# A hybrid decoder step on one core: in which order the weight sums are made, and which engine does the small two-operand arithmetic

## The chip, the core and the metric

The kernel runs on one core of a Trainium2 chip. A core has a matrix engine (TensorE, PE in the profile), VectorE (DVE), ScalarE (ACT), GpSimd (POOL) and a queue engine (SyncE, SP); each works through its own list of instructions in order and waits on semaphores for the others. PEld is TensorE's loading of weights, DMA the transfer engines that move data between DRAM and the core's memory. DMAs are issued from SP and, the adding ones in this kernel, from GpSimd. The metric is the time of one execution on the device in microseconds; the time before is the median of three runs.

## The reference

One layer with two token mixers beside each other, over 512 prompt tokens and 8 x 4 sampled tokens (544 columns in all), in float32:

```python
z = x @ w_in                                   # 1024 -> a_val, a_gate, b_x, b_gate, g_a, g_b
u = a_val * jax.nn.sigmoid(a_gate)
ua = jnp.concatenate([ctx_a, u], axis=1)
ca = jax.nn.silu(layer_norm(causal_dwconv(ua, w_dw_a, b_dw_a), ln_a_g, ln_a_b))   # 31 taps
y_a = ca @ w_proj_a
ub = jnp.concatenate([ctx_b, b_x], axis=1)
cb = causal_dwconv(ub, w_dw_b, b_dw_b)                                            # 4 taps
hs, h_last = rg_lru(cb, h0, w_rg_a, b_rg_a, w_rg_x, b_rg_x, rg_lam, reset_first)
y_b = (hs.astype(x.dtype) * jax.nn.gelu(b_gate)) @ w_proj_b
mix = (jax.nn.sigmoid(g_a) * y_a + jax.nn.sigmoid(g_b) * y_b) @ w_out
x1 = layer_norm(DN_ALPHA * x + mix, ln1_g, ln1_b)
ff = jnp.square(jax.nn.relu(x1 @ w_ff1)) @ w_ff2
ple = jax.nn.sigmoid(x1 @ w_ple_gate) * (p @ w_ple_proj)
y = layer_norm(DN_ALPHA * x1 + ff + ple, ln2_g, ln2_b)
```

In `rg_lru`, r and ig are sigmoids of two block-diagonal products of cb; a = exp(-8 r softplus(-lam)), the input is sqrt(1 - a^2) * ig * cb, and h is the running sum h = a h + input over the tokens.

## The kernel before

Channels lie on the 128 partitions and tokens along the free axis, so one channel tile is 128 x 544. Every matrix product is made of three passes over operands that are split into a high and a low part: ScalarE copies a weight chunk `raw` (128 x 1024) to `hi`, VectorE subtracts to get `lo`, and TensorE multiplies hi by hi, hi by lo and lo by hi. One chunk feeds 48 matmuls.

The order of the products is the string `ORDER`: "a" is the gated input of the 31-tap convolution, "x" that of the 4-tap one, "r" the two block-diagonal products (two groups of five channel tiles), "g", "b" and "c" the gates, "p" the product with `w_proj_b` and "q" that with `w_proj_a`. Then come `w_out`, the first layer norm, the embedding gate, the feed-forward layers (FF below) and the last norm.

Beside the products run steps that VectorE, ScalarE and GpSimd take when a planner finds room. `Clocks` keeps a modelled time for each engine, `put` hands in a sequence of steps with a priority and a due chunk, `fill` takes the next ones up to 1.5 us ahead of TensorE's modelled time, and `need` forces what is due. The list that each engine then works through is fixed when the program is built. The largest such work is `queue_conv_a`: for each of the eight channel tiles, four `products` (128 x 248) with two sums over them for the sampled tokens, then 30 taps (`tap`, ca<-u,par_a,ca, 128 x 482 to 511) on VectorE for the prompt tokens. `last` adds the finished tile to `sum_a`. When all eight are in, `lna` (the convolution's layer norm) starts: `lnash` and `lnasl` are the split of sum_a, and lnamu is the matmul on TensorE that makes the mean. The chain from there to `cas`, the input of "q", runs while TensorE does the rest of "p" and part of the gates.

`conv_b_sample` makes the 4-tap convolution of the sampled tokens (tiles cbs, seven instructions of 128 x 64 and two of 128 x 32 for two channel tiles). `rg_group` multiplies the sigmoid `gg` by `cb` as soon as ScalarE has made it, and `scan` multiplies `gate` by the scan's result. Two-operand arithmetic in all of these is issued on GpSimd (`G`), beside its small copies (ctx_a, ctx_b, tb, st_u, hl).

The feed-forward layers are done with seven products in place of eight, for which some weight blocks are sums of others (S3, S1, S2, S4). These sums are made in DRAM beside the earlier stages: a DMA from SP copies one block to a scratch tile, and a DMA from GpSimd (`accum_op=add`) adds a second block, S3 for S2, and S2 for S4. There are 92 of them. `sum_stream` says when: the k-th add falls due when TensorE's modelled time reaches `SUM_FROM + k * SUM_EVERY`, and its copy `COPY_AHEAD` adds earlier. The feed-forward stage loads the sums as `fraw<-sum_S`.

```python
def sum_stream(e):
    k = (clocks.t["T"] - SUM_FROM) / SUM_EVERY
    if e == "D" and to_copy and n_adds - len(to_copy) < k + COPY_AHEAD:
        return 0.0, copy_one
    if e == "G" and to_add and len(to_copy) < len(to_add) and n_adds - len(to_add) < k:
        return 0.0, add_up
```

All compute is issued through one helper, so nearly every row of the profile carries line L155; rows are told apart by tile names.

Of the kernel before, what the change touches and what calls it, by code (L numbers as in the profile page):

```python
# [20 lines left out]
CK, RK = 31, 4  # L21
# [12 lines left out]
PANELS = [(1, p, None) for p in (1, 2, 3)]  # L34
for _g, _ps in enumerate(((4, 5, 6), (7, 8, 9), (10, 11, 12, 13), (14, 15))):
    PANELS += [(2, _p, _g) for _p in range(4)] + [(1, _p, None) for _p in _ps]
SUM_FROM, SUM_EVERY, COPY_AHEAD = 40.0, 6.0, 3
RAW_BUFS = 3
SPLIT_BUFS = 4
LOAD_AHEAD = 5  # L40
# [119 lines left out]
def tile_hybrid_step(ctx: ExitStack, tc: tile.TileContext, I, O):  # L160
# [72 lines left out]

    lead = [LEAD]
    sums, summed_up, to_copy, to_add = {}, set(), deque(), deque()
    for kind, n in [(1, p) for p in (1, 2, 3)] + [(2, p) for p in range(4)] + [(1, p) for p in range(4, 16)]:
        w = I["w_ff1" if kind == 1 else "w_ff2"][n]
        ncol = 512 if kind == 1 else 6 * P
        for c in range(kind):
            cs = slice(c * ncol, c * ncol + ncol)  # L240
            s = {nm: dpool.tile([P, ncol], F32, name=f"sum{kind}_{n}_{c}_{nm}") for nm in ("S3", "S1", "S2", "S4")}
            for nm, own, src in (("S3", w[0, :, cs], w[2, :, cs]), ("S1", w[2, :, cs], w[3, :, cs]),
                                 ("S2", w[3, :, cs], s["S3"]), ("S4", w[1, :, cs], s["S2"])):
                sums[kind, n, c, nm] = s[nm]
                to_copy.append(lambda to=s[nm], own=own: DMA.dma_start(to, own))
                to_add.append((lambda to=s[nm], src=src: G.dma_start(to, src, accum_op=OP.add, max_dma_last_dim=1024),
                               (kind, n, c, nm)))
    n_adds = len(to_add)

# [463 lines left out]

    sg, u, ca = [None] * 8, [None] * 8, [None] * 8
    sum_a = [None]

    todo = []

# [15 lines left out]
    def queue_conv_a(ct):  # L734
        def wk(k):
            return par_a[:, k, ct:ct + 1]
        prod = {}

        def products():
            for t in range(NS):  # L740
                if t % 2 == 0:
                    prod[t // 2] = apool.tile([P, NB, 2, CK], F32, tag="act", name=f"prod{ct}_{t}")
                G.tensor_mul(prod[t // 2][:, :, t % 2, :], ctx_a[ct // 2][:, ct % 2, :, t:t + CK],
                             par_a[:, 0:CK, ct].unsqueeze(1).to_broadcast([P, NB, CK]))

        def reduce(t):
            cv = conv_s[:, ct, :].rearrange("p (b t) -> p b t", t=NS)
            V.tensor_reduce(cv[:, :, 2 * t:2 * t + 2], prod[t], op=OP.add, axis=AX.X)

        def first():  # L750
            ca[ct] = act(f"ca{ct}")
            S.activation(ca[ct][:, :SEQ], u[ct][:, :SEQ], AF.Identity, scale=wk(CK - 1), bias=A("b_dw_a", ct))
            S.activation(ca[ct][:, SEQ:], conv_s[:, ct, :], AF.Identity, bias=A("b_dw_a", ct))

        def tap(k):
            s = CK - 1 - k
            V.scalar_tensor_tensor(ca[ct][:, s:SEQ], u[ct][:, :SEQ - s], wk(k), ca[ct][:, s:SEQ],
                                   op0=OP.mult, op1=OP.add)

        def last():  # L760
            if sum_a[0] is None:
                sum_a[0] = act("sum_a")
                G.tensor_copy(sum_a[0], ca[ct])
            else:
                G.tensor_add(sum_a[0], sum_a[0], ca[ct])

        may_start = lambda: 0.0 if len(summed) >= ct // 2 * 2 - 1 else INF
        steps = [("G", products, may_start), ("V", lambda: reduce(0)), ("V", lambda: reduce(1)), ("S", first)]
        steps += [("V", lambda k=k: tap(k)) for k in range(CK - 1)]
        put(3 + 0.1 * (ct // 2), steps + [("G", last)] + [("V", lambda: summed.append(ct))],  # L770
            PROJ_A - CONV_DUE)

    summed = []
# [70 lines left out]
    def conv_b_sample(c0):  # L844

        ws = R_OFF["w_dw_b"]
        acc_, t = (cpool.tile([P, 2, NB, NS], F32, tag=f"cbs{i}", name=f"cbs{i}_{c0}", bufs=1) for i in range(2))
        for k in range(RK):
            w = par_r[:, ws + k, c0:c0 + 2].unsqueeze(2).unsqueeze(3).to_broadcast([P, 2, NB, NS])
            G.tensor_mul(t if k else acc_, ctx_b[:, c0:c0 + 2, :, k:k + NS], w)  # L850
            if k:
                G.tensor_add(acc_, acc_, t)
        for j in range(2):
            G.tensor_scalar(cb[c0 + j][:, SEQ:].rearrange("p (b t) -> p b t", t=NS), acc_[:, j], R("b_dw_b", c0 + j),
                            None, op0=OP.add)

    tb = cpool.tile([P, 10, RK - 1], F32, name="tb")
# [11 lines left out]
    def rg_group(g):  # L869
        b0 = 5 * g  # L870

        def prod(mt, w, isx):
# [10 lines left out]
            else:  # L883
                gg[ct] = act(f"gg{ct}")
                S.activation(gg[ct], tok(ps), AF.Sigmoid, bias=R("b_rg_x", ct))
                G.tensor_mul(gg[ct], gg[ct], cb[ct])
            fill()

        def decay_act(mt):
# [10 lines left out]
        def scan(mt):  # L900
# [4 lines left out]
            def last():  # L905
                V.tensor_tensor_scan(sq[ct], aa[ct], gg[ct], 0.0, op0=OP.mult, op1=OP.add)
                G.tensor_copy(hl[:, ct, :], sq[ct][:, SEQ - 1::NS])
                G.tensor_mul(gate[ct], gate[ct], sq[ct])

            def part(p):  # L910
                if p == 0:
# [137 lines left out]

    def evac_proja(mt, ps, h):  # L1050
        V.tensor_mul(sa[mt], tok(ps), sa[mt])
        (G if mt < 6 else V).tensor_add(sa[mt], sa[mt], sb[mt])

        def keep(parts_):
            mix[mt] = parts_
# [663 lines left out]
```

## Time and profile before

| | us |
|---|---|
| three runs | 1013.59, 1014.58, 1017.05 |
| median | 1014.58 |
| the profiled execution | 1010.48 |
| its span, first to last instruction | 1008.7 |
| TensorE busy | 935.5 (93%) |
| VectorE busy | 793.7 (79%) |
| ScalarE busy | 496.1 (49%) |
| GpSimd busy | 254.2 (25%) |

Busy is time with at least one instruction in the engine. The profile is of one execution, 4.1 us faster than the median of the runs. Instructions of one engine overlap at their ends: a row's mean duration is longer than the spacing of a run of such instructions.

### The profile page before, as it was taken

To read this page: it belongs to the slowest core of one execution; us is meant where nothing else is said; L and a number is where in the kernel's file an instruction comes from. 1 tells how busy PE (TensorE), PEld (TensorE's weight loads), DVE (VectorE), ACT (ScalarE), POOL (GpSimd) and SP (SyncE) were. 2 spreads that over 40 slices of the span, in tenths; PEclk is the share of its full clock that TensorE was granted. 3 is DMA by queue.
4 is the path that set the end of the run, shared out by engine and by line. 5 is a ranking of instruction groups with operands and counts; after the bars stand their busy time and mean duration, and the time that the engine had idled before them with its cause. 6 is when DMAs were issued, how large, how long until landed. Compare 5 with 4: busy or idle time off the path is not lost.

```text
span 1008.7 us, 18589 instructions
## 1 busy us (share of the span) xinstructions
PE 935.5 (93%) x7236; PEld 924.7 (92%) x7236; DVE 793.7 (79%) x1337; ACT 496.1 (49%) x875; POOL 254.2 (25%) x265
## 2 busy tenths in 40 slices
PE   8999798975989797999999999999999999999895
PEld 8999798975979797999999999989999899989895
DVE  5799999899997998793356883979688686777547
ACT  6422236623449622562233772775674655854601
POOL 0453755675637621210421211000000000000002
PEclk9999988997989899999999999999999999999998
DMA  8557689875889594967869784446546446446412
GB/s 298 147 152 185 180 200 262 196 175 138 183 214 202 136 212 130 229 160 196 260 155 253 173 225 54 149 133 188 174 138 204 148 146 218 147 144 204 133 48 84
DMA packets 125272, 175.81 MB, mean 174 GB/s; under 512 B 9920, under 2 KB 97344, under 8 KB 124224
## 3 DMA queue, kind: packets, MB, share of 16 engines
q1 hardware_dynamic: 96064, 146.31, 45.0%
q0 software_dynamic: 29120, 28.32, 20.3%
q8 instruction: 57, 0.93, 0.4%
q14 instruction: 31, 0.25, 0.1%
HBM read 167.57 MB, written 60.44 MB: 226 GB/s over the span
## 4 chain that ended last, share of the span: by engine, by line
PE 47%; DVE 29%; DMA 7%; ACT 7%; issue 5%; POOL 4%; SPq 0%; DVEq 0%; POOLq 0%; ACTq 0%
PE psq L155 13%; PE ps L155 13%; DVE ca L155 11%; PE f L155 8%; PE g L155 6%; DVE lo L155 4%; ACT fy L155 2%; ACT fhi L155 1%; DMA fraw<-sum_S 1%; DMA sum_S<-in_w_ff_dram 1%; DVE flo L155 1%; PE pps L155 1%; DVE th L155 1%; ACT fz L155 1%; DMA sum_S<-sum_S 1%
## 5 line engine op out<-in xcount | busy, mean ns | idle before, releaser
L155 DVE SCALAR_TENSOR_TENSOR ca<-u,par_a,ca 128x482 f32<-128x482 f32 (+29 forms) x240 | 176.3, 792 | 0.3
L155 ACT ACTIVATE hi<-raw 128x1024 fp32r<-128x1024 f32 (+3 forms) x109 | 99.9, 929 | 130.3 <-PE ps L155 52.6
L155 ACT ACTIVATE fhi<-fraw 128x512 fp32r<-128x512 f32 (+1 forms) x229 | 124.3, 571 | 60.5 <-DMA fraw<-sum_S 21.7
L155 DVE TENSOR_TENSOR flo<-fraw,fhi 128x512 fp32r<-128x512 f32 (+1 forms) x229 | 138.2, 620 | 17.7 <-ACT fhi L155 17.4
L155 DVE TENSOR_TENSOR lo<-raw,hi 128x1024 fp32r<-128x1024 f32 (+3 forms) x105 | 122.2, 1178 | 25.4 <-ACT hi L155 25.4
L155 POOL TENSOR_TENSOR y<-y,rows_g 128x512 f32<-128x512 f32 x2 | 3.1, 1550 | 379.1 <-ACT y L155 379.1
L155 POOL DMA_DIRECT2D sum_S<-sum_S x46 | 45.3, 985 | 171.5 <-DMA sum_S<-sum_S 91.2
L155 PE MATMUL f<-x1h,fhi 128*128 128x272 f32 x212 | 59.6, 294 | 5.1 <-DVE fz L155 3.5
L155 POOL DMA_DIRECT2D sum_S<-in_w_ff_dram x46 | 51.8, 1198 | 28.5 <-DMA sum_S<-in_w_ff_dram 27.1
L155 PE MATMUL f<-x1h,flo 128*128 128x272 f32 x212 | 58.6, 289 | 0.2 <-DVE flo L155 0.2
L155 PE MATMUL f<-x1l,fhi 128*128 128x272 f32 x212 | 58.4, 288 | 0.0
L155 PE MATMUL ps<-x0h,hi 128*128 128x288 f32 x104 | 23.9, 313 | 29.6 <-ACT gate L155 14.6
L155 PEld LDWEIGHTS ps<-x0h,hi 128*128 128x128 f32 x104 | 16.9, 200 | 31.5 <-ACT gate L155 15.5
L155 PEld LDWEIGHTS f<-x1h,fhi 128*128 128x128 f32 x212 | 39.0, 189 | 7.3 <-DVE fz L155 5.4
L155 DVE TENSOR_TENSOR acc<-acc,g 128x272 f32<-128x272 f32 x80 | 34.8, 434 | 12.9 <-PE g L155 12.1
L155 PEld LDWEIGHTS f<-x1h,flo 128*128 128x128 f32 x212 | 38.9, 188 | 0.5 <-DVE flo L155 0.5
L155 PEld LDWEIGHTS f<-x1l,fhi 128*128 128x128 f32 x212 | 39.0, 189 | 0.0
L155 PE MATMUL psq<-x1l,hi 128*128 128x288 f32 (+1 forms) x128 | 36.9, 288 | 0.0
L155 PE MATMUL psq<-x1h,lo 128*128 128x288 f32 (+1 forms) x128 | 36.8, 288 | 0.0
L155 PE MATMUL psq<-x1h,hi 128*128 128x288 f32 (+1 forms) x128 | 36.8, 288 | 0.0
L155 POOL TENSOR_TENSOR prod<-ctx_a,par_a 128x248 f32<-128x248 f32 x32 | 30.9, 1150 | 0.0
L155 ACT ACT_TABLE_LOAD x20 | 25.7, 1283 | 1.1 <-PEq L1709 0.7
(1994 smaller groups left out, 3385.9 us busy)
## 6 DMA issues: line engine op xcount, KB each, us to landing
raw<-in_w_in_dram SPq DMA_DIRECT2D x51, 512.0 KB, 5.0
fraw<-in_w_ff_dram SPq DMA_DIRECT2D x65, 256.0 KB, 3.5
sum_S<-in_w_ff_dram SPq DMA_DIRECT2D x60, 256.0 KB, 5.3
fraw<-sum_S SPq DMA_DIRECT2D x60, 256.0 KB, 3.3
sum_S<-in_w_ff_dram SPq DMA_DIRECT2D x32, 384.0 KB, 5.8
fraw<-sum_S SPq DMA_DIRECT2D x64, 192.0 KB, 2.9
fraw<-in_w_ff_dram SPq DMA_DIRECT2D x48, 192.0 KB, 3.1
sum_S<-in_w_ff_dram POOLq DMA_DIRECT2D x30, 256.0 KB, 5.4
```

Source lines behind the costliest of these rows:

```text
L155: return fn(out, *args, **kw)
```

## The change

The constants of the sums change, and their order: panels are taken in seven sets of three or four, and within a set all S3 are made, then all S1, all S2 and all S4. The two-operand instructions of GpSimd go to VectorE, all but four at the very end of the program. The first tile of `sum_a` is no longer copied: the first add takes two tiles.

```diff
-SUM_FROM, SUM_EVERY, COPY_AHEAD = 40.0, 6.0, 3
+SUM_FROM, SUM_EVERY, COPY_AHEAD = 25.0, 7.2, 4
...
-    for kind, n in [(1, p) for p in (1, 2, 3)] + [(2, p) for p in range(4)] + [(1, p) for p in range(4, 16)]:
...
+    SETS = ([(1, p, 0) for p in (1, 2, 3)], [(2, p, 0) for p in range(4)], [(1, p, 0) for p in (4, 5, 6)],
+            [(1, p, 0) for p in (7, 8, 9)], [(2, p, 1) for p in range(4)], [(1, p, 0) for p in (10, 11, 12)],
+            [(1, p, 0) for p in (13, 14, 15)])
+    for ps_ in SETS:
+        for nm in ("S3", "S1", "S2", "S4"):
+            for kind, n, c in ps_:
...
-                G.tensor_mul(prod[t // 2][:, :, t % 2, :], ctx_a[ct // 2][:, ct % 2, :, t:t + CK],
+                V.tensor_mul(prod[t // 2][:, :, t % 2, :], ctx_a[ct // 2][:, ct % 2, :, t:t + CK],
...
             if sum_a[0] is None:
+                first_ca.append(ct)
+                sum_a[0] = True
+            elif sum_a[0] is True:
                 sum_a[0] = act("sum_a")
-                G.tensor_copy(sum_a[0], ca[ct])
+                V.tensor_add(sum_a[0], ca[first_ca[0]], ca[ct])
             else:
-                G.tensor_add(sum_a[0], sum_a[0], ca[ct])
+                V.tensor_add(sum_a[0], sum_a[0], ca[ct])
...
-        steps = [("G", products, may_start), ("V", lambda: reduce(0)), ("V", lambda: reduce(1)), ("S", first)]
+        steps = [("V", products, may_start), ("V", lambda: reduce(0)), ("V", lambda: reduce(1)), ("S", first)]
...
-            G.tensor_mul(t if k else acc_, ctx_b[:, c0:c0 + 2, :, k:k + NS], w)
+            V.tensor_mul(t if k else acc_, ctx_b[:, c0:c0 + 2, :, k:k + NS], w)
             if k:
-                G.tensor_add(acc_, acc_, t)
+                V.tensor_add(acc_, acc_, t)
...
-            G.tensor_scalar(cb[c0 + j][:, SEQ:].rearrange("p (b t) -> p b t", t=NS), acc_[:, j], R("b_dw_b", c0 + j),
+            V.tensor_scalar(cb[c0 + j][:, SEQ:].rearrange("p (b t) -> p b t", t=NS), acc_[:, j], R("b_dw_b", c0 + j),
...
-                G.tensor_mul(gg[ct], gg[ct], cb[ct])
+                V.tensor_mul(gg[ct], gg[ct], cb[ct])
...
-                G.tensor_mul(gate[ct], gate[ct], sq[ct])
+                V.tensor_mul(gate[ct], gate[ct], sq[ct])
...
-        (G if mt < 6 else V).tensor_add(sa[mt], sa[mt], sb[mt])
+        V.tensor_add(sa[mt], sa[mt], sb[mt])
```

First place: GpSimd's list in the first 50 us, before and then after. A row `sum1_2_0_S3<-in_w_ff1_dram` is the adding DMA of form S3 of panel 2; `S2<-...S3` reads an earlier sum.

```order
L155 DMA sum1_1_0_S3_101<-in_w_ff1_dram 256x256
L155 DMA sum1_1_0_S1_102<-in_w_ff1_dram 256x256
L155 DMA sum1_1_0_S2_103<-sum1_1_0_S3_101 256x256
L155 COPY st_u_269<-u2_801 128x30
L155 COPY ctx_a1_260<-u2_801 128x8x4
L155 COPY st_u_269<-u3_833 128x30
L155 COPY ctx_a1_260<-u3_833 128x8x4
L155 DMA sum1_1_0_S4_104<-sum1_1_0_S2_103 256x256
```

```order
L155 DMA sum1_3_0_S1_106<-in_w_ff1_dram 256x256
L155 COPY ctx_b_264<-bx0_935 128x8x4
L155 COPY tb_284<-bx0_935 128x3
L155 COPY ctx_b_264<-bx1_970 128x8x4
L155 COPY tb_284<-bx1_970 128x3
L155 DMA sum1_1_0_S2_107<-sum1_1_0_S3_101 256x256
L155 DMA sum1_2_0_S2_108<-sum1_2_0_S3_102 256x256
L155 DMA sum1_3_0_S2_109<-sum1_3_0_S3_103 256x256
```

Before, an S2 stands one add behind the S3 that it reads, and the next copies behind that; after, five adds lie between a panel's S3 and its S2.

Second place: VectorE's list at the first group of block-diagonal products, before and then after. `u` is the last convolution input, `lo` and `hi` of 128x896 and 32x384 the split of the group's second weights.

```order
L155 TENSOR_TENSOR u_1891<-ps_1_1758,sg_1755 128x544
L155 TENSOR_TENSOR lo_1909<-raw_1724,hi_1824 128x896
L155 TENSOR_TENSOR hi_1895<-raw_1769,hi_1895 32x384
L155 SCALAR_TENSOR_TENSOR ca_1417<-u_801,par_a,ca_1417 128x495
L155 SCALAR_TENSOR_TENSOR ca_1594<-u_833,par_a,ca_1594 128x493
```

```order
L155 TENSOR_TENSOR u_1881<-ps_1_1748,sg_1745 128x544
L155 TENSOR_TENSOR gg_1896<-gg_1896,cb_939 128x544
L155 TENSOR_TENSOR gg_1913<-gg_1913,cb_974 128x544
L155 TENSOR_TENSOR gg_1931<-gg_1931,cb_1375 128x544
L155 TENSOR_TENSOR gg_1947<-gg_1947,cb_1410 128x544
L155 TENSOR_TENSOR gg_1961<-gg_1961,cb_1537 128x544
L155 TENSOR_TENSOR lo_1964<-raw_1694,hi_1816 128x896
L155 TENSOR_TENSOR hi_1885<-raw_1757,hi_1885 32x384
```

The five multiplies that stood on GpSimd's list now stand in a row on VectorE's, ahead of the next weight split; the second group has the same five.

Third place: TensorE's list around lnamu, before and then after.

```order
L155 MATMUL ps_0_4359<-hb6h,lo_4300 128x256
L155 MATMUL lnamu_4454<-lnash,ones 128x288
L155 MATMUL lnamu_4454<-lnasl,ones 128x288
L155 MATMUL lnamu_4460<-lnash,ones 128x256
L155 MATMUL lnamu_4460<-lnasl,ones 128x256
L155 MATMUL ps_0_4359<-hb7h,hi_4227 128x288
```

```order
L155 MATMUL ps_0_4497<-hb6h,lo_4523 128x256
L155 MATMUL lnamu_4590<-lnash,ones 128x288
L155 MATMUL lnamu_4590<-lnasl,ones 128x288
L155 MATMUL lnamu_4594<-lnash,ones 128x256
L155 MATMUL lnamu_4594<-lnasl,ones 128x256
L155 MATMUL ps_0_4497<-hb7h,hi_4399 128x288
```

The mean's four matmuls stand at row 2660 of TensorE's list before and at row 2780 after: 120 matmuls of "p" go ahead of them. All other rows of TensorE keep their order, but for the four of the variance, which move back likewise.

## Rows read from the trace of the kernel before

**Rows 1.** Windows: busy us and counts by engine, TensorE's clock, DMA, four stages.
```profile
0.00:40.00 40.00, 37.32 (x276) 36.48 (x277) 21.21 (x29) 23.24 (x30) 8.69 (x22) 1.00 0.68 234
40.00:400.30 360.30, 316.51 (x2402) 313.40 (x2400) 341.64 (x465) 155.96 (x212) 191.16 (x191) 0.94 0.78 184
400.30:620.00 219.70, 219.08 (x1719) 218.22 (x1720) 144.75 (x259) 101.52 (x182) 48.10 (x50) 0.99 0.79 196
620.00:1008.70 388.70, 362.62 (x2845) 356.62 (x2844) 286.05 (x586) 215.39 (x452) 6.30 (x4) 0.99 0.47 147
```
**Rows 2.** Waits of TensorE, 100 to 400.5 us: total, times, longest.
```profile
PE ps L155 <- ACT gate L155: 14.6, 3, 12.1
...
PE lnamu L155 <- ACT lnash L155: 6.3, 1, 6.3
```
**Rows 3.** Windows, the same columns: behind two of TensorE's waits, and an undisturbed stretch.
```profile
126.30:132.20 5.90, 5.89 (x26) 5.89 (x27) 5.90 (x9) 4.60 (x7) 4.34 (x7) 0.50 0.98 185
...
400.30:405.40 5.10, 5.10 (x21) 4.90 (x22) 5.10 (x13) 3.43 (x8) 1.41 (x3) 0.50 0.71 143
60.00:100.00 40.00, 40.00 (x321) 40.00 (x321) 40.00 (x56) 12.43 (x15) 19.69 (x25) 1.00 0.69 172
```
**Rows 4.** Timeline of VectorE, 80 to 92 us: start, length, instruction, count.
```profile
80.44 0.71 DVE L155 TENSOR_TENSOR cb1l<-cb,cb1h 128x544 fp32r<-128x544 f32 x1
81.07 3.97 DVE L155 SCALAR_TENSOR_TENSOR ca<-u,par_a,ca 128x496 f32<-128x496 f32 x6
```
**Rows 5.** Timeline of VectorE, 154 to 165 us.
```profile
156.03 9.31 DVE L155 SCALAR_TENSOR_TENSOR ca<-u,par_a,ca 128x495 f32<-128x495 f32 x6
```
**Rows 6.** Timeline of GpSimd, 154 to 165 us.
```profile
155.56 8.61 POOL L155 TENSOR_TENSOR gg<-gg,cb 128x544 f32<-128x544 f32 x5
```
**Rows 7.** GpSimd by operation, 33.4 to 401 us: busy, mean ns, idle before.
```profile
L155 POOL TENSOR_TENSOR prod<-ctx_a,par_a 128x248 f32<-128x248 f32 x32 | 30.9, 1150 | 0.0
...
L155 POOL TENSOR_TENSOR gate<-gate,th 128x544 f32<-128x544 f32 x10 | 19.8, 1980 | 0.0
L155 POOL TENSOR_TENSOR gg<-gg,cb 128x544 f32<-128x544 f32 x10 | 18.1, 1841 | 11.8 <-ACT gg L155 11.8
...
L155 POOL COPY ctx_b<-bx 128x32 f32<-128x32 f32 x10 | 15.2, 1521 | 9.1 <-ACT bx L155 9.1
L155 POOL TENSOR_TENSOR sum_a<-sum_a,ca 128x544 f32<-128x544 f32 x7 | 12.5, 1781 | 15.5 <-DVE ca L155 14.4 <-DVE aa L155 1.0
```
**Rows 8.** Timeline of VectorE, 104 to 112 us.
```profile
105.19 5.34 DVE L155 SCALAR_TENSOR_TENSOR ca<-u,par_a,ca 128x510 f32<-128x510 f32 x2
```
**Rows 9.** Timeline of VectorE, 218 to 246 us.
```profile
222.89 5.27 DVE L155 TENSOR_TENSOR t<-aa,par_r 128x8 f32<-128x8 f32 x1
...
242.95 0.17 DVE L155 TENSOR_TENSOR t<-aa,par_r 128x8 f32<-128x8 f32 x1
```
**Rows 10.** Timeline of VectorE, 400 to 405 us.
```profile
402.10 1.51 DVE L155 TENSOR_TENSOR ca<-ca,lnamu 128x288 f32<-128x288 f32 x4
```
**Rows 11.** Waits of VectorE, 40 to 400.5 us: total, times, longest.
```profile
DVE conv_s L155 <- POOL prod L155: 4.0, 2, 3.0
DVE lnasl L155 <- ACT lnash L155: 3.1, 1, 3.1
```
**Rows 12.** Tile gg, 140 to 175 us: duration ns min/median/max, first and last start.
```profile
L155 ACT ACTIVATE gg<-rg,par_r x5: 704/715/717, 151.4 to 157.8; 128x544 f32<-128x544 f32 x5
```
**Rows 13.** Timeline of GpSimd, 28 to 36 us.
```profile
29.55 0.21 POOL L155 COPY st_u<-u 128x30 f32<-128x30 f32 x1 [28.05 <-DVE u L155]
```
**Rows 14.** Timeline of GpSimd, 178 to 192 us.
```profile
180.32 5.68 POOL L155 COPY ctx_b<-bx 128x32 f32<-128x32 f32 x1 [1.80 <-ACT bx L155]
```
**Rows 15.** Waits of all engines, whole span.
```profile
POOL sum_S L155 <- DMA sum_S<-sum_S: 91.2, 16, 9.9
```
**Rows 16.** Windows, columns as above: either side of the feed-forward stage's start.
```profile
560.00:620.00 60.00, 60.00 (x484) 60.00 (x484) 45.12 (x100) 36.15 (x81) 11.96 (x14) 1.00 0.77 178
620.00:680.00 60.00, 56.30 (x439) 54.77 (x439) 48.26 (x99) 39.32 (x85) 0.00 (x0) 1.00 0.40 118
```

More of the change, by code (lines that the diff above doesn't have):

```diff
@@ L235, in tile_hybrid_step @@
     sums, summed_up, to_copy, to_add = {}, set(), deque(), deque()
-    for kind, n in [(1, p) for p in (1, 2, 3)] + [(2, p) for p in range(4)] + [(1, p) for p in range(4, 16)]:
[L237 to L246, printed above, removed]
+    SETS = ([(1, p, 0) for p in (1, 2, 3)], [(2, p, 0) for p in range(4)], [(1, p, 0) for p in (4, 5, 6)],
[4 more added lines that the diff above has]
+            for kind, n, c in ps_:
+                w = I["w_ff1" if kind == 1 else "w_ff2"][n]
+                ncol = 512 if kind == 1 else 6 * P
+                cs = slice(c * ncol, c * ncol + ncol)
+                s = sums[kind, n, c, nm] = dpool.tile([P, ncol], F32, name=f"sum{kind}_{n}_{c}_{nm}")
+                own, src = {"S3": (0, w[2, :, cs]), "S1": (2, w[3, :, cs]), "S2": (3, sums.get((kind, n, c, "S3"))),
+                            "S4": (1, sums.get((kind, n, c, "S2")))}[nm]
+                to_copy.append(lambda to=s, own=w[own, :, cs]: DMA.dma_start(to, own))
+                to_add.append((lambda to=s, src=src: G.dma_start(to, src, accum_op=OP.add, max_dma_last_dim=1024),
                                (kind, n, c, nm)))
@@ L715, in tile_hybrid_step @@
     sum_a = [None]
+    first_ca = []
     todo = []
@@ L761, in last @@
             if sum_a[0] is None:
+                first_ca.append(ct)
+                sum_a[0] = True
+            elif sum_a[0] is True:
                 sum_a[0] = act("sum_a")
-                G.tensor_copy(sum_a[0], ca[ct])
+                V.tensor_add(sum_a[0], ca[first_ca[0]], ca[ct])
             else:
-                G.tensor_add(sum_a[0], sum_a[0], ca[ct])
+                V.tensor_add(sum_a[0], sum_a[0], ca[ct])
         may_start = lambda: 0.0 if len(summed) >= ct // 2 * 2 - 1 else INF
-        steps = [("G", products, may_start), ("V", lambda: reduce(0)), ("V", lambda: reduce(1)), ("S", first)]
+        steps = [("V", products, may_start), ("V", lambda: reduce(0)), ("V", lambda: reduce(1)), ("S", first)]
         steps += [("V", lambda k=k: tap(k)) for k in range(CK - 1)]
-        put(3 + 0.1 * (ct // 2), steps + [("G", last)] + [("V", lambda: summed.append(ct))],
+        put(3 + 0.1 * (ct // 2), steps + [("V", last)] + [("V", lambda: summed.append(ct))],
             PROJ_A - CONV_DUE)
```

## The prediction

> **What bounds the kernel now.** I read the windows by stage first, then TensorE's waits, then VectorE's and GpSimd's timelines beside each other. In the feed-forward stage and from 400 to 620 us TensorE is busy 363 of 389 and 219 of 220 us [rows 1]: little is to be had there. The loss is from 40 to 400 us: TensorE is busy 316.5 of 360.3 us, idle 43.8, and VectorE is busy 341.6 [rows 1]. At full clock TensorE did 321 matmuls in 40 us, 8.03 per us [rows 3], so its 2402 matmuls [rows 1] need 299 us; it took 61 us more. Most of the difference is waiting: 12.1 us at one place for a chain that ends in gate, 6.3 us at the end for lnash [rows 2]. The rest is the clock: after each of six such waits the granted clock was 0.50, the 1.2 GHz level, for some us more (5.9 us behind the first, 5.1 behind the last) [rows 3].
>
> Why VectorE is full is the second reading. Six taps in a row took 3.97 us when GpSimd did no arithmetic, so 0.65 each [rows 4]. Six taps beside five gg multiplies took 9.31 us [rows 5], while the five took 8.61 us [rows 6]: the two engines alternated, and each multiply cost VectorE (9.31 - 3.97)/5 = 1.07 us. The four products of one tile did the same: two taps took 5.34 us [rows 8], 4.0 more than their own 1.3, and a small multiply of 0.17 us took 5.27 [rows 9] with products and a sum_a add beside it. So work put on GpSimd here is paid by VectorE, at more than VectorE's own price: a subtraction of the same 128 x 544 takes 0.63 us there (start to start, 80.44 to 81.07) [rows 4].
>
> So the end of this stage is set by VectorE's list up to lnamu, and I count on that list.
>
> **The change part by part.** All terms go against the profiled execution, 1010.48 us (span 1008.7 and 1.8 around it); the median of the runs is 4.1 us longer, which I add at the end.
>
> *Stalls that go.* gg: 10 x 1.07 = 10.7 us. gate: 10 of like size and mean length [rows 7], some beside idle time of VectorE: 9. sum_a: 7 adds, 7. Products: 32 in eight groups of four [rows 7]; two groups come before 40 us, one met a VectorE that was waiting for it [rows 11], the other five at 2.7 to 4.0 (the upper end from [rows 8]): 17. Together 44, bounds 38 and 50. VectorE's own work up to lnamu is then 341.6 - 44 = 297.6 us.
>
> *Work that comes to VectorE.* 24 products of 128 x 248 behind 40 us: four subtractions of 256 and 288 columns took 1.51 us [rows 10], so 0.33 each, 7.9. The eight earlier ones fall where VectorE is busy 21 of 40 us [rows 1] and cost nothing; that cover gone, 2.6. The 45 small ones of conv_b_sample: 8 columns take 0.17 [rows 9], 544 take 0.71 [rows 4], about 1 ns a column between them; for 32 and 64 columns 0.2, as most wait for the one before: 9. The 27 of 128 x 544 (10 gg, 10 gate, 7 sum_a): 0.66, 17.8. Together 35, bounds 31 and 42. The six adds on `sa` fall behind 460 us, where VectorE has room: nothing (4 us if it had not).
>
> *lnamu stands 120 matmuls later on TensorE.* That takes 120/8.03 = 14.9 us of work out of what follows lnamu, and puts some three more weight splits and evictions ahead of it on VectorE: 3 us.
>
> *Waits.* VectorE was idle 360.3 - 341.6 = 18.7 us, and its waits name GpSimd or a ScalarE step behind a GpSimd one: 4.0 on products, 3.1 on lnash behind sum_a [rows 11], and ScalarE's halves of cb behind cbs. These mostly go. New ones come, as VectorE's list is in order. In each of the two groups five gg multiplies stand ahead of the next weight split; ScalarE made the five gg over 151.4 to 157.8 us and 0.7 [rows 12], 7.1 us against 3.2 of multiplies: up to 3.9 us of waiting, behind which lo and the taps stand, and TensorE waits for lo. And cbs now waits on VectorE for GpSimd's copy ctx_b, five times, 0.7 each. I take 12 us of idle time in all (8 and 3.5 and a remainder), bounds 1.3 and 55 (below).
>
> *lnamu.* It comes at 40 + 297.6 + 35 + 3 + 12 = 387.6 us against 400.3: 12.7 earlier. TensorE could have been there at 40 + 2522/8.03 = 354, so VectorE still sets it. With the 14.9 us, and 2.6 for the half clock behind lnamu (5.1 us at 0.50 [rows 3]) when the long wait is gone, 30.2 us. The norm's chain behind lnamu has 55 us of matmuls as cover before "q" needs it (counted in the order), 70 before; TensorE, busy 219 of 220 us there [rows 1], was never kept by it. I cost it at nothing; if it comes late, 5.
>
> *The order of the sums.* GpSimd stood 91.2 us for an S3 or S2 of the same panel [rows 15]. Nothing on another engine waits for an add itself, so its end brings only that the copies queued behind are not held up. Ten adds now come after the feed-forward stage has begun, over 538 matmuls or 67 us, where there were none; in the order each sum is first loaded 180 us or more of matmuls behind its add, so none is late. But they share the DMA: 0.77 busy before the stage's start, 0.40 behind it [rows 16]. With sums in it I expect about 0.8 there, as in the first stage, and weight loads that come later, as SP's list has the sums' copies between them: 2 us, bounds 0 and 8. At the start three copies go ahead of SP's sixth weight chunk; with DMA busy 0.68 up to 40 us [rows 1] and five chunks ahead of it that costs nothing, or 3.
>
> Sum: 1010.5 - 30.2 + 2 = 982.3; at the median, 986.
>
> **A rule against the change.** The alternation above has five multiplies of 8.61 us beside six taps [rows 5, 6]. The Trainium skill, SBUF — State Buffer, "Who interferes with whom", has it that a VectorE instruction with two SBUF inputs and a GpSimd instruction that reads SBUF hold a shared port in turn, each for its whole length, and the later one is blocked. By that rule the copies left on GpSimd, which read SBUF too, are held off all the more when VectorE has 35 us more of such work; the trace agrees: a copy of 0.21 us beside an idle VectorE [rows 13], and one of 5.68 [rows 14].
>
> **Rivals.** *The copies hold VectorE.* ctx_b's ten copies took 15.2 us [rows 7], and cbs now waits for them on VectorE. Against it: VectorE is late and rarely there first, and while it waits a copy is short. If they count in full: 986 + 15 = 1001.
>
> *TensorE nearly bounds the stage.* All waits of VectorE go but 1.3 us of gaps, the stalls were 50 and the new work 31: lnamu at 40 + 291.6 + 31 + 3 + 1.3 = 367, 20.7 earlier than above, no loss on the sums: 963. For it: most waits named GpSimd; against it: the five gg in a row.
>
> *VectorE takes over GpSimd's waits.* This is the slower side. GpSimd waited 11.8 us for gg and 9.1 for bx [rows 7]; on VectorE nobody would do taps meanwhile. With these in full, the copies' 15.2 and its old 18.7, idle time is 54.8, 42.8 more than I took: 1029. It becomes slower than before from 40 us of idle time on, over twice what there is now. Against it: GpSimd was early for those waits, and VectorE will be late.
>
> *Nothing is won.* The stage's end is set by weight loads and clock, not by VectorE: 1012 to 1017. Against it: VectorE is 95% busy and its stalls are plain.
>
> **How the numbers follow.** My forecast 0.62, with its own range 972 to 1000; copies 0.15; TensorE bound 0.10; VectorE waits 0.08; nothing 0.05. The range 964 to 1008 holds the first three but their outer ends, and leaves out the last two. No change, within 0.3% (3 us, about what can be told apart here), is 0.05; slower 0.08; faster 0.87.
>
> **What would show it.** Right: taps at 0.65 us each throughout to lnamu, VectorE busy some 335 us from 40 us to lnamu and lnamu at about 388; GpSimd busy under 100 us; no wait for a sum of the same panel; VectorE idle a few us at each row of five gg. Wrong: lnamu later than 400; waits of VectorE for GpSimd's copies; long waits of TensorE for fhi from 590 to 660 us.

## The result, and the profile after

The changed kernel takes 1005.08 us (median of 4 runs, 1004.12 to 1007.80) against 1014.09 us for the kernel before beside it: a ratio of 0.991, 95% interval 0.988 to 0.994. It is faster, by 9 us where 28 were forecast. The profiled execution took 1004.12 us, its span 1002.3.

The page and the windows of the changed kernel, in the columns of [rows 1], with the stages cut at the new lnamu (399.1 us) and at the new first matmul of the feed-forward layers (f0). f0 was at 627.7 and is at 616.4; [rows 1] cuts at 620, so the last line is the stretch from lnamu to f0 in the kernel before:

```profile
PE 938.7 (94%) x7236; PEld 927.5 (93%) x7236; DVE 794.6 (79%) x1447; ACT 493.5 (49%) x874; POOL 139.1 (14%) x154
...
0.00:40.00 40.00, 37.81 (x274) 36.50 (x275) 20.61 (x47) 23.23 (x30) 5.88 (x18) 1.00 0.89 280
40.00:399.10 359.10, 329.39 (x2522) 326.68 (x2521) 342.87 (x557) 156.78 (x216) 86.22 (x89) 0.96 0.71 172
399.10:616.40 217.30, 209.97 (x1657) 208.89 (x1655) 147.64 (x266) 99.75 (x183) 31.86 (x33) 0.99 0.76 187
616.40:1002.30 385.90, 361.52 (x2788) 355.48 (x2788) 283.47 (x581) 213.77 (x448) 15.09 (x14) 0.97 0.54 161
```
```profile
400.30:627.70 227.40, 225.79 (x1774) 224.72 (x1775) 146.96 (x265) 103.24 (x187) 48.10 (x50) 0.99 0.77 190
```

GpSimd is at 86 us in the second stage, under the 100 that were to show the move right, and TensorE does 2522 matmuls from 40 us to lnamu, 120 more than before, as the order said. But lnamu is at 399.1, not at 387.6. VectorE was busy 342.9 us where 335.6 were forecast (7.3 more) and idle 359.1 - 342.9 = 16.2 us where I took 12 (4.2 more): together the 11.5 us. And from lnamu to f0 it took 217.3 us, 10.1 less than before and not 17.5 less: TensorE, which was idle for 227.4 - 225.8 = 1.6 us of that stretch before, was idle for 7.3.

VectorE's list from 40 to 400 us by operation (busy us, mean ns of one, idle before; the mean counts the overlap with the next instruction, the busy time does not):

```profile
L155 DVE SCALAR_TENSOR_TENSOR ca<-u,par_a,ca 128x482 f32<-128x482 f32 (+28 forms) x240 | 160.3, 734 | 0.2
L155 DVE TENSOR_TENSOR prod<-ctx_a,par_a 128x248 f32<-128x248 f32 x32 | 18.7, 658 | 0.0
L155 DVE TENSOR_TENSOR gate<-gate,th 128x544 f32<-128x544 f32 x10 | 7.3, 725 | 0.3
L155 DVE TENSOR_TENSOR gg<-gg,cb 128x544 f32<-128x544 f32 x10 | 7.1, 723 | 4.3 <-ACT gg L155 4.3
L155 DVE TENSOR_TENSOR cbs<-ctx_b,par_r 128x64 f32<-128x64 f32 x20 | 4.0, 222 | 3.4 <-POOL ctx_b L155 3.0
```

Every tap now costs about what an undisturbed one cost in [rows 4]: 160.3/240 = 0.67 us each. The two rows of five gg cost 4.3 us of waiting together, the copies of ctx_b 3.0. What is off is one line: 32 products, not 24 (none came before 40 us), at 18.7/32 = 0.58 us each, not 0.33.

What VectorE (40 to 399 us) and TensorE (120 to 400 us) waited for in the changed kernel (us in total, times, longest), and what GpSimd did before the longest of these waits, 161.6 to 170.2 us:

```profile
DVE lo L155 <- ACT hi L155: 6.6, 2, 4.2
...
PE rg L155 <- ACT th L155: 9.3, 2, 8.6
```
```profile
124.54 3.69 POOL L155 DMA_DIRECT2D sum_S<-in_w_ff_dram  x3
146.53 0.64 POOL L155 COPY st_u<-u 128x30 f32<-128x30 f32 x1 [18.31 <-DVE u L155]
147.11 0.70 POOL L155 COPY ctx_a<-u 128x32 f32<-128x32 f32 x1
149.72 0.64 POOL L155 COPY st_u<-u 128x30 f32<-128x30 f32 x1 [1.90 <-DVE u L155]
150.30 0.70 POOL L155 COPY ctx_a<-u 128x32 f32<-128x32 f32 x1
150.95 4.95 POOL L155 DMA_DIRECT2D sum_S<-in_w_ff_dram  x4
153.96 2.95 POOL L155 DMA_DIRECT2D sum_S<-sum_S  x1
```

GpSimd stood 18.3 us in front of a copy whose input VectorE had not made yet and 1.9 us in front of the next one, and the five adds that stood behind them all went out at once. The DMAs issued from 145 to 175 us landed so late (KB each, median us from issue to landing):

```profile
raw<-in_w_in_dram SPq DMA_DIRECT2D x4, 512.0 KB, 15.0
sum_S<-in_w_ff_dram POOLq DMA_DIRECT2D x4, 384.0 KB, 13.4
...
sum_S<-sum_S POOLq DMA_DIRECT2D x1, 384.0 KB, 22.1
```

A load of these weights (`raw`, 512 KB) takes 5.1 us in the median of the whole run; here it took 15. `th`, for which TensorE waited, stood on ScalarE behind the split (`hi`) of such a load. The same happens at the output projection, on GpSimd and then on VectorE:

```profile
510.43 0.42 POOL L155 COPY sum<-res 128x288 f32<-128x288 f32 x1 [25.31 <-DVE res L155]
510.90 3.86 POOL L155 DMA_DIRECT2D sum_S<-sum_S  x4
```
```profile
525.29 1.29 DVE L155 TENSOR_TENSOR lo<-raw,hi 128x512 fp32r<-128x512 f32 x2 [7.41 <-ACT hi L155]
```

So there are two suspects: the price of a product (theory 1), and adds that go out in bunches behind a copy that waits (theory 2). The rivals are that nobody waits for the products, that the sums' bytes and not their bunching make loads late, and that the order of the sums was the gain.

### The profile page after: what moved, and what is told of

It reads as the page before. It is cut to its first block, busy times and chain, and to the rows that moved or that the text cites. A ratio compares the mean times of both kernels' runs of the same rounds, so it can differ in the third digit from the quotient of the medians.

```text
span 1002.3 us, 18587 instructions
## 1 busy us (share of the span) xinstructions
PE 938.7 (94%) x7236; PEld 927.5 (93%) x7236; DVE 794.6 (79%) x1447; ACT 493.5 (49%) x874; POOL 139.1 (14%) x154
## 4 chain that ended last, share of the span: by engine, by line
PE 47%; DVE 31%; ACT 7%; DMA 7%; issue 5%; POOL 2%; SPq 0%; DVEq 0%; ACTq 0%; POOLq 0%
PE ps L155 13%; PE psq L155 12%; DVE ca L155 9%; PE f L155 9%; DVE lo L155 5%; PE g L155 5%; DMA raw<-in_w_in_dram 2%; DVE cb L155 2%; ACT fhi L155 2%; ACT fy L155 2%; DVE th L155 2%; POOL st_u L155 1%; DMA raw<-in_w_ple_gate_dram 1%; DVE prod L155 1%; DMA fraw<-in_w_ff_dram 1%
## 5 line engine op out<-in xcount | busy, mean ns | idle before, releaser
L155 DVE SCALAR_TENSOR_TENSOR ca<-u,par_a,ca 128x482 f32<-128x482 f32 (+28 forms) x240 | 160.3, 734 | 0.2
L155 DVE TENSOR_TENSOR lo<-raw,hi 128x1024 fp32r<-128x1024 f32 (+3 forms) x105 | 112.5, 1082 | 28.2 <-ACT hi L155 28.2
L155 POOL DMA_DIRECT2D sum_S<-in_w_ff_dram x46 | 48.0, 1361 | 137.9 <-DMA sum_S<-in_w_ff_dram 131.5
L155 POOL COPY st_u<-u 128x30 f32<-128x30 f32 x8 | 17.9, 2233 | 68.9 <-DVE u L155 68.9
L155 PEld LDWEIGHTS ps<-x0h,hi 128*128 128x128 f32 x104 | 16.2, 192 | 10.2 <-ACT gate L155 4.0
```

Of the source, the lines that this page charges most:

```text
L155: return fn(out, *args, **kw)
```

## The experiments

All are compared with the kernel before on the same chip. lnamu, the time from there to f0, and that from f0 to the last matmul of `f` are of one profile each; rows_arith and rows_arith_res are the same program up to 500 us and have lnamu 4 us apart, so I take sizes from the medians and from busy times, and use these columns for where a difference lies. The kernels ran on several chips, whose medians of the kernel before differ by 2 us, so it is the ratios that compare between rows.

| kernel | median us | ratio to before [95%] | lnamu | to f0 | f |
|---|---|---|---|---|---|
| before | 1014.1 to 1016.0 | | 400.3 | 227.4 | 315.2 |
| the change | 1005.1 | 0.991 [0.988, 0.994] | 399.1 | 217.3 | 319.7 |
| rows | 996.0 | 0.980 [0.977, 0.982] | 392.3 | 215.8 | 316.6 |
| arith_only | 995.4 | 0.980 [0.978, 0.982] | 393.5 | 216.9 | 319.0 |
| sums_only | 1023.1 | 1.007 [1.004, 1.009] | 405.4 | 232.7 | 318.5 |
| res_act | 998.8 | 0.983 [0.979, 0.986] | 400.7 | 211.9 | 317.6 |
| copies_act | 993.0 | 0.977 [0.975, 0.979] | 391.9 | 212.3 | 318.6 |
| rows_arith | 988.6 | 0.973 [0.970, 0.975] | 388.9 | 211.7 | 319.5 |
| rows_arith_res | 991.0 | 0.975 [0.973, 0.977] | 393.0 | 211.5 | 320.3 |
| rows_arith_copies | 984.3 | 0.969 [0.967, 0.971] | 386.5 | 213.4 | 317.4 |
| rows_copies | 984.7 | 0.970 [0.968, 0.972] | 381.9 | 211.7 | 320.3 |
| prod_gpsimd | 1005.3 | 0.989 [0.987, 0.991] | 395.1 | 223.4 | 319.8 |

### The price of a product: rows, stride2, stride4

```diff
-par_a = cpool.tile([P, NA, 8], F32, name="par_a")     # out["par_a"] = per_channel(...)
+par_a = cpool.tile([P, 8, NA], F32, name="par_a")     # ... .transpose(0, 2, 1)
...
-    par_a[:, 0:CK, ct].unsqueeze(1).to_broadcast([P, NB, CK])
+    par_a[:, ct, 0:CK].unsqueeze(1).to_broadcast([P, NB, CK])
```

> The changed kernel, with the table par_a laid out with a channel's weights side by side (128x8xNA in place of 128xNAx8), so that a product of the sample convolution reads its 31 weights contiguously and not one in every 32 bytes. Nothing else is different; VectorE issues the same instructions in the same order. Theory: a product takes 0.57 us in the changed kernel in place of the forecast 0.33 because of that stride; then it falls to 0.33 to 0.38, VectorE has 6 to 7.5 us less to do ahead of the first mean of the first normalisation (lnamu), lnamu comes at 391 to 393 (399.1), and the kernel takes about 998 us (1005). Rival: the short rows of 31 numbers set the price, then a product stays at 0.55 to 0.6 and the time within 2 us of 1005. Second rival: the products do become short, but VectorE only waits longer for late weight loads, and the time stays above 1002.

Four products one after the other in the changed kernel, and then in rows:

```profile
41.02 2.34 DVE L155 TENSOR_TENSOR prod<-ctx_a,par_a 128x248 f32<-128x248 f32 x4
```
```profile
41.92 1.40 DVE L155 TENSOR_TENSOR prod<-ctx_a,par_a 128x248 f32<-128x248 f32 x4
```

All 32 of them, and TensorE's wait for th, in rows:

```profile
L155 DVE TENSOR_TENSOR prod<-ctx_a,par_a 128x248 f32<-128x248 f32 x32 | 11.1, 412 | 0.0
```
```profile
PE rg L155 <- ACT th L155: 9.2, 2, 8.8
```

Theory 1 holds: 11.1 us for all 32 in place of 18.7, lnamu at 392.3, 996 us. An instruction's length runs on past the start of the next: 2.34 is three starts of 0.57 and a last 0.63, and 1.40 is three of 0.33 and a last 0.41. So contiguous weights give the forecast 0.33 us. The second rival falls too: the late loads stayed (TensorE still waited 8.8 us for th) and the time came back all the same.

In stride2 and stride4 the table is cut as [P, 4, NA, 2] and [P, 2, NA, 4].

> The changed kernel with the weights of two channels interleaved (128x4xNAx2), so that a product reads one weight in every 8 bytes; in the changed kernel it is one in every 32 bytes (0.57 us a product), in rows they are contiguous (0.33 us). Theory: the price comes with the distance, because weights 32 bytes apart lie each in a piece of its own: at 8 bytes 0.33 to 0.40 us. Rival: any distance but the next number costs the same: 0.55 to 0.58 us.

> As stride2 with four channels interleaved (128x2xNAx4), one weight in every 16 bytes. Theory: the price comes with the distance: 0.33 to 0.50 us a product, not less than in stride2. Rival: any distance but the next number costs the same: 0.55 to 0.58 us.

The tile prod in the changed kernel (32 bytes from weight to weight), in rows (4), in stride2 (8) and in stride4 (16): duration ns min/median/max, first and last start.

```profile
L155 DVE TENSOR_TENSOR prod<-ctx_a,par_a x32: 603/657/715, 41.0 to 341.8; 128x248 f32<-128x248 f32 x32
```
```profile
L155 DVE TENSOR_TENSOR prod<-ctx_a,par_a x32: 402/412/418, 41.9 to 335.2; 128x248 f32<-128x248 f32 x32
```
```profile
L155 DVE TENSOR_TENSOR prod<-ctx_a,par_a x32: 398/404/413, 42.3 to 336.0; 128x248 f32<-128x248 f32 x32
```
```profile
L155 DVE TENSOR_TENSOR prod<-ctx_a,par_a x32: 593/617/654, 41.6 to 338.4; 128x248 f32<-128x248 f32 x32
```

The price does come with the distance, but in one step: two weights in 16 bytes cost nothing extra, one in 16 bytes costs 0.2 us a product, one in 32 hardly more (0.24). My range for stride4, 0.33 to 0.50 us, was too low (0.62 by length, 0.53 from start to start). Each of the two ran once beside the others, at 1000.0 and 1000.3 us; I read nothing from these times.

### One half of the change at a time: arith_only, sums_only

```diff
 # arith_only: the changed kernel, with the sums' loop of the kernel before and
-SUM_FROM, SUM_EVERY, COPY_AHEAD = 25.0, 7.2, 4
+SUM_FROM, SUM_EVERY, COPY_AHEAD = 40.0, 6.0, 3
 # sums_only: the kernel before, with the changed kernel's SETS loop and
-SUM_FROM, SUM_EVERY, COPY_AHEAD = 40.0, 6.0, 3
+SUM_FROM, SUM_EVERY, COPY_AHEAD = 25.0, 7.2, 4
```

> The arithmetic moved to VectorE as in the change, the sums of panels with the order, start and period of the kernel before (each second-form add right behind the third-form add that it waits for). Theory: the change's sums cost part of what the arithmetic gains, because copies on GpSimd that wait for VectorE hold back the adds queued behind them, which then go out five or four at once (at 151 and 511 us) and delay weight loads; with the sums as before adds are held apart by their own data, the weight loads around 157 and 512 us land within 10 us, TensorE's wait of 8.6 us at 161.6 shrinks to under 4, VectorE's idle 7.4 us at 518 goes, lnamu comes at 393 to 396, f0 some 210 us behind it, and the kernel takes 990 to 996 us. Rival: the sums' new order is what made the gain, then 1008 us or more. Second rival: adds that wait for data hold the small copies behind them, and VectorE waits for these: 1000 to 1006.

> Only the sums changed (sets of panels, form by form, start 25, period 7.2, four copies ahead); GpSimd keeps its products, sums and gates as in the kernel before. Theory: VectorE's stalls beside GpSimd's arithmetic (44 us over what the same instructions take alone) stay, so that lnamu does not come earlier than 400, and adds held behind waiting copies add late loads: 1012 to 1022 us. Rival: the sums' order is the gain of the change, because GpSimd no longer waits for the third form's landing: lnamu under 396 and 1006 us or less.

The time of arith_only is as theory 2 has it; that of sums_only, 1023.1 us, is 1 us above its range. The rival that the sums' order made the gain is out: alone, the sums cost 0.7%, and taken out of the change they give 10 us. In arith_only GpSimd comes to the same copies early as well, but behind them two adds go out and the next is held for 10 us by its own data; the weight loads of 145 to 175 us land in 9.1 us in the median:

```profile
150.73 1.21 POOL L155 DMA_DIRECT2D sum_S<-in_w_ff_dram  x1
151.50 1.46 POOL L155 DMA_DIRECT2D sum_S<-sum_S  x1
163.15 0.95 POOL L155 DMA_DIRECT2D sum_S<-sum_S  x1 [10.20 <-DMA sum_S<-sum_S]
```

In sums_only VectorE is slow beside GpSimd as before and the bunch is there as well, behind the five gg that GpSimd still makes (start and length; GpSimd from 157 to 171 us):

```profile
157.26 0.65 POOL L155 COPY st_u<-u 128x30 f32<-128x30 f32 x1 [12.57 <-DVE u L155]
...
161.58 8.66 POOL L155 TENSOR_TENSOR gg<-gg,cb 128x544 f32<-128x544 f32 x5
170.19 5.01 POOL L155 DMA_DIRECT2D sum_S<-in_w_ff_dram  x4
```

Two points of arith_only missed. TensorE's longest wait for th was 4.6 us, not under 4. And f0 came 216.9 us behind lnamu, not 210: an add still stood behind the copy of `res`, but the same adds stand there in rows_arith below, which needs 211.7, so what kept arith_only is not shown. Besides, f took 319.0 us though not one add falls into it (POOL 0.00 in the window of that stretch):

```profile
610.40:929.40 319.00, 306.67 (x2363) 301.80 (x2364) 246.61 (x509) 197.69 (x420) 0.00 (x0) 0.98 0.52 162
```

### What holds the adds: res_act, copies_act

```diff
-            G.tensor_copy(st, r)                       # res_act: this one only
+            S.activation(st, r, AF.Copy)
-        G.tensor_copy(st_u[:, mt, :], u[mt][:, SEQ - (CK - 1):SEQ])
+        S.activation(st_u[:, mt, :], u[mt][:, SEQ - (CK - 1):SEQ], AF.Copy)
...                                                     # copies_act: ctx_a, ctx_b, tb and hl likewise
```

> The changed kernel with one edit: the two copies that begin the sum for the first normalisation behind the output projection (sum<-res, one for each half) are made by ScalarE and not by GpSimd. Theory: GpSimd's queue stood 25.3 us behind the first of them, and the four adds behind it went out together at 511 us and delayed three weight loads by some 5 us; without the copy each add goes out when its own data is there, no load waits for a bunch, VectorE's idle 7.4 us at 518 falls under 3, f0 comes 210 to 212 us behind lnamu (217.3), and the kernel takes 998 to 1000 us (1005). Rival: the loads are late because of the bytes of the sums in that stretch, however they are spread: f0 216 to 218 us behind lnamu, and 1004 to 1006 us.

> The changed kernel (sums in sets, weights strided) with one edit: every small copy that waits for VectorE or ScalarE (st_u, ctx_a, ctx_b, tb, hl and the start of the sum) is made by ScalarE, so that nothing but their own data holds the adds in GpSimd's queue. Theory: it was the copies in front of them, not the sets, that sent the adds out in bunches; then the loads at 157 and 512 us are no longer late, and the time is that of arith_only, whose adds are held apart by their data, 995 us, or a little better: 990 to 996. Rival: sets of sums ask for more at a time, however they are queued, and weight loads are late as before: 1001 to 1006 us.

In res_act the adds around 510 us go out when their own data is there:

```profile
497.92 0.95 POOL L155 DMA_DIRECT2D sum_S<-sum_S  x1 [8.19 <-DMA sum_S<-in_w_ff_dram]
503.50 0.95 POOL L155 DMA_DIRECT2D sum_S<-sum_S  x1 [4.63 <-DMA sum_S<-in_w_ff_dram]
508.26 0.95 POOL L155 DMA_DIRECT2D sum_S<-sum_S  x1 [3.82 <-DMA sum_S<-in_w_ff_dram]
518.84 0.95 POOL L155 DMA_DIRECT2D sum_S<-sum_S  x1 [9.63 <-DMA sum_S<-in_w_ff_dram]
```

f0 comes 211.9 us behind lnamu, and two copies of 0.4 and 0.6 us moved to another engine are worth 6 us. With all 48 copies gone from GpSimd the other bunch is gone too: in copies_act the loads of 145 to 175 us land in 5.2 us, TensorE's wait of 8.6 us is not there, and VectorE, whose work is the same (344.5 us busy), is idle 351.9 - 344.5 = 7.4 us and not 16.2.

```profile
raw<-in_w_in_dram SPq DMA_DIRECT2D x5, 512.0 KB, 5.2
sum_S<-sum_S POOLq DMA_DIRECT2D x3, 384.0 KB, 7.0
```
```profile
PE rg L155 <- ACT th L155: 0.9, 2, 0.7
```
```profile
40.00:391.90 351.90, 329.73 (x2519) 326.58 (x2518) 344.54 (x567) 162.20 (x257) 42.08 (x44) 0.97 0.71 175
391.90:604.20 212.30, 208.65 (x1657) 207.76 (x1655) 147.65 (x265) 100.77 (x185) 30.83 (x31) 1.00 0.77 191
```

The sums are the same 92 in the same sets, and the four writes of ctx_a to DRAM (272 KB each) still go out at 151 us, as in the change; so it is the bunching, and not the sums' number or order, that made loads late. Not all of copies_act's gain is that: VectorE's 3.0 us of waiting for ctx_b are gone with the copies too.

### Both together: rows_arith, rows_arith_res, rows_arith_copies, rows_copies

> The arithmetic moved, the sums as in the kernel before, and the table of weights laid out so that a product reads its 31 weights contiguously (the edits of arith_only and of rows together). Theory: the two costs are separate, a product's stride (lnamu 6.9 us earlier in rows, the kernel 9 us faster) and adds that go out in bunches (lnamu 5.6 us earlier in arith_only, the kernel 10 us faster), so they add: lnamu at 386 to 388 (the forecast was 387.6), the kernel 986 to 990 us. Rival: both take away the same wait, that of VectorE and TensorE for the weight loads at 157 to 175 us, and only one of them counts: lnamu at 391 to 393 and 994 to 996 us.

988.6 us and lnamu at 388.9, a little behind the range for it: the two costs are separate and nearly add (9 and 10 us alone, 16.5 together).

> As rows_arith, and the two copies that begin the sum for the first normalisation made by ScalarE and not by GpSimd. Theory: with the adds no longer behind a copy that waits for VectorE, f0 comes 210 to 212 us behind lnamu (res_act: 211.9; arith_only, where one add and a pair still stood behind that copy: 216.9), and all that the forecast had missed but the last stage is back: 981 to 985 us. Rival: with the sums in their old order the adds are apart already and the copy's place does nothing: within 2 us of rows_arith.

Wrong: 991.0 us. f0 does come 211.5 us behind lnamu, but so it does in rows_arith (211.7), with the copy still on GpSimd: with the sums in their old order, moving it brings nothing. The rival came closer, though 991.0 us lies 2.4 us above rows_arith and not within 2.

> As rows_arith, with every small copy that waits for VectorE or ScalarE (st_u, ctx_a, ctx_b, tb, hl and the start of the sum) made by ScalarE, so that GpSimd's queue holds adds alone behind the first stage. Theory: copies held off beside VectorE's arithmetic (one of 0.6 us took 11.8 us) delay VectorE little, about 3 us of idle time in all, and ScalarE has room for 48 copies of 0.1 to 0.3 us: lnamu at 384 to 387 and 979 to 984 us. Rival: in ScalarE's queue the same copies stand ahead of gates and splits that VectorE and TensorE wait for, or adds that nothing holds back any more crowd the loads: 986 us or more.

> As copies_act, with the table of weights laid out contiguously. Theory: with the products at 0.33 us and the adds free, the change as it was meant gives what was forecast: lnamu at 384 to 388, 982 to 987 us, the same as rows_arith_copies (984.3), since the order of the sums by itself is then worth nothing. Rival: the sets cost some of the loads their time, and it stays 4 us or more behind rows_arith_copies, at 988 or more.

984.3 us, just over its range, and 984.7 us, within it; lnamu of rows_copies, at 381.9, is earlier than expected. The two times are equal: with the copies away and the weights contiguous, the order of the sums makes no difference that shows. These are the fastest versions, 3% under the kernel before and 2% under the change. In rows_copies the second and the third stage read:

```profile
40.00:381.90 341.90, 326.84 (x2517) 324.20 (x2515) 336.76 (x565) 162.34 (x257) 42.09 (x44) 0.97 0.73 180
381.90:593.60 211.70, 208.56 (x1656) 207.68 (x1654) 147.60 (x265) 100.59 (x185) 30.84 (x31) 1.00 0.78 192
```

VectorE is busy 336.8 us, the 335.6 of the forecast, and idle 5.1.

### Was the move of the products worth it at that price: prod_gpsimd

```diff
-                V.tensor_mul(prod[t // 2][:, :, t % 2, :], ...      # steps: ("V", products, may_start)
+                G.tensor_mul(prod[t // 2][:, :, t % 2, :], ...      # steps: ("G", products, may_start)
```

> As arith_only (weights strided, sums as before), with the 32 products of the sample convolution left on GpSimd as in the kernel before. VectorE is spared 32 times 0.57 = 18 us; the stalls of its taps beside these products come back. Theory: VectorE lost 44 us beside some 115 us of GpSimd's arithmetic, 0.38 us for each us, so 31 us of products give 12 us of stalls and the 4 us of waiting for them come back: the move of the products, at their strided price, was worth nothing, lnamu at 391 to 396 and 993 to 998 us. Rival: stalls come only where taps and a product meet, and there every us of GpSimd costs VectorE about one: 31 us against 18 saved, lnamu past 404 and 1006 us or more. Second rival: the stalls stem from the other arithmetic, then lnamu at 380 and 982 us.

The stalls were right (13 us where 12 were expected) and the time was not. It is near the first rival's, but not for its reason, as lnamu is at 395.1 and not past 404. The 240 taps take 13 us longer than in the changed kernel (160.3); the 14 taps that overlap a product have all of that excess. The lines of 40 to 400 us, and the windows:

```profile
L155 DVE SCALAR_TENSOR_TENSOR ca<-u,par_a,ca 128x482 f32<-128x482 f32 (+29 forms) x240 | 173.3, 782 | 2.0 <-ACT ca L155 1.9
...
L155 POOL TENSOR_TENSOR prod<-ctx_a,par_a 128x248 f32<-128x248 f32 x25 | 29.3, 1302 | 1.9 <-PE rg L155 1.9
```
```profile
40.00:395.10 355.10, 320.29 (x2430) 316.11 (x2429) 340.32 (x537) 157.09 (x213) 112.33 (x123) 0.95 0.81 193
```

lnamu comes at 395.1 as expected, but after 2430 matmuls; in arith_only it was at 393.5 after 2529. That is 99/8.03 = 12 us of TensorE's work less, which is left for later (from lnamu to f0 it takes 223.4 us and not 216.9), and 1005.3 us in place of 995.4. So even at 0.57 us a product VectorE was the better place.

## Why the prediction was wrong

It was right in sign and in what went away, and 19 us too hopeful at the median. Between the profiled executions the miss is 1004.1 - 982.3 = 21.8 us: lnamu came 11.5 us later than forecast, the stretch from lnamu to f0 shrank by 7.4 us less, and what follows f0 grew by 4.9 us and not by 2. Its steps in order:

*Stalls that go: 44 (38 to 50).* Right in kind. VectorE was busy 341.6 us before; the two-operand work that came adds 48 (18.7, 7.3, 7.1 and 4.0 in the rows above, 5.8 for the rest of conv_b_sample, 5.0 for sum_a), the splits and evictions 3 by my count, and it was busy 342.9: some 48 to 50 us of stalls went, near the upper bound. That these were more than forecast made up for part of the next error; that is luck.

*New work: 35 (31 to 42).* **Here the sum failed first.** It was some 46 from start to start, and nearly all of the difference is the products: 32 at 0.57, some 18 us, where I had 24 x 0.33 = 7.9. Two things were wrong in that term. All products come behind 40 us. And I priced them by subtractions of 256 and 288 columns whose operands are contiguous [rows 10], while a product reads one weight in every 32 bytes; that could be read in the code, `par_a[:, 0:CK, ct]` of a tile 128 x NA x 8. Contiguous weights bring the 0.33 us and some 9 us of the kernel's time. The rest of the term (9 for the small ones, 17.8 for the large) was within 1 us. The Trainium skill has the rule that I passed over: SBUF — State Buffer, "Door 1: The DMA port swizzle", says that SBUF is read in lines of 16 bytes and that a stream wants at least two hits in a line. The runs agree for strides of 8 bytes (404 ns) and 16 (617). The Trainium skill also says there that four fp32 are free to stride over, and here they are not (617 ns); the measurement decides: two are (404).

*Idle time of VectorE: 12.* 16.2. The two parts that I named, gg and ctx_b, are there with 4.3 and 3.0 (8 and 3.5 were taken). The rest is mostly a wait I had not named: 6.6 us for `hi`, behind two of the weight loads that came late.

*The order of the sums: nothing ahead of lnamu, 2 us in the feed-forward layers.* **This step failed too, in its reason:** a term put at nothing cost some 10 us. "Nothing on another engine waits for an add itself" is true, but I followed only the copies behind the adds and not the adds behind the copies. Before, GpSimd came to a copy late, after its own arithmetic; the ten copies of ctx_b waited 9.1 us for their input [rows 7]. Now it comes early and stands there (ctx_b 56.9 us, st_u 59.3 where it had been 26.4):

```profile
L155 POOL COPY st_u<-u 128x30 f32<-128x30 f32 x6 | 17.4, 2908 | 59.3 <-DVE u L155 59.3
L155 POOL COPY ctx_b<-bx 128x32 f32<-128x32 f32 x10 | 11.8, 1205 | 56.9 <-ACT bx L155 56.9
```

Either half of the change brings GpSimd there early: in sums_only, where it keeps its arithmetic but no longer waits for an S3, ctx_b's copies wait 36.4 us, and in arith_only, without the arithmetic, 33.9. What makes the bunch is the sets: adds that the planner had spread by its clock pile up behind these copies and go out together, since in a set three or four in a row wait for nothing of each other. In the old order an S2 waits for its own S3 [rows 15], and that keeps most adds apart (in arith_only a load issued at 289.5 us, behind two adds, still took 12.2 us). Taking the copies out of that queue is worth 12 us (copies_act), undoing the sets 10 us (arith_only). That the adds cost 2 us in the feed-forward layers is not shown: f takes 319.7 us with adds in it, 319.0 without any (arith_only), 315.2 before.

*lnamu to f0: 17.5 less.* 10.1. The second bunch, at 511 us, took most of the rest: without it 15.5 less (res_act). The half clock behind lnamu went, as forecast, but after a wait behind that bunch another came, with a granted clock of 0.50 (1.2 GHz) from 532.5 to 535.9 us.

*The rule against the change.* It held, and cost little. A copy of GpSimd's was held off for 11.8 us beside VectorE's taps, but VectorE waited only 3.0 us for ctx_b; the price lay with the adds queued behind the copies.

Of the rivals, "copies hold VectorE" (1001) came nearest by its number, and that is luck: VectorE waited only 3.0 us for the copies; the weight loads behind the adds behind them did it, and the products. (The TensorE rival's 963 lies just outside the range that was said to hold it.) Take both causes away (rows_copies) and the kernel is at 984.7 us, with 336.8 us of work on VectorE, where 986 and 335.6 were forecast. So the two steps above are what the forecast lacked. That the numbers agree to 2 us is partly luck: rows_copies moves the copies as well, more stalls went and more work came than forecast, and lnamu 5.7 us earlier than forecast makes up for a smaller gain to f0 (15.7 and not 17.5) and 5.3 us more behind it, where 2 were forecast.

What stays open is the feed-forward layers: f takes 316.6 to 320.3 us in every other kernel of the table and 315.2 before:

```profile
627.70:942.90 315.20, 302.24 (x2363) 297.55 (x2364) 246.44 (x509) 198.12 (x420) 0.00 (x0) 1.00 0.53 164
```

TensorE does the same 2363 matmuls there and is idle for about as long (13.0 us before, 11.2 to 14.6 in the others), with the same three waits of 1.7 us each; but it is busy for 304 to 308 us in place of 302.2, and its granted clock is 0.98 or 0.99 where it was 1.00. So most of the difference is the clock. What lowers it is not known; I tried nothing on that.

## What to carry to other kernels

Price an instruction that moves to another engine by its own operands, stride and all, and not by the nearest shape; if it reads a table across, lay the table out anew first. When work leaves an in-order engine, ask what that engine will now arrive at early: a wait that its own work used to cover, and what stands in the queue behind it; DMAs that are spread by a plan need something real between them. Count a stage by what the bounding engine has done up to a mark as well as by the time of the mark, since a planner moves the mark.

## What the runs showed of the hardware that was not expected

- VectorE, 128 x 248 in fp32 with one operand strided: 412 ns contiguous, 404 at 8 bytes, 617 at 16, 657 at 32.
- A 128 x 30 copy on GpSimd, 0.21 us beside an idle VectorE [rows 13], lasted 11.8 us while VectorE went without a pause through two splits and 15 taps; it ended when VectorE next stood idle, at 69.1 us. The Trainium skill, SBUF — State Buffer, "Who interferes with whom", has one of the two engines hold a shared port pair for a whole instruction while the other is blocked; that one copy was kept out through 17 of VectorE's instructions in a row is what the trace adds:

```profile
57.29 11.84 POOL L155 COPY st_u<-u 128x30 f32<-128x30 f32 x1
```

- Five adding DMAs of 384 KB whose issue began within 3 us landed 13.4 us (median of the four from the weights) and 22.1 us (the last) after issue, and 512 KB loads issued on another queue before they had landed needed 15.0 us (median) in place of 5.1. With the adds apart (copies_act) these were 7.0 us and 5.2.
